# The state-space preparation on VectorE instead of GpSimd, a unit in three pieces

## The chip, the cores and the metric

The kernel runs on one core of a Trainium2 chip. The metric is the time of one execution on the device in microseconds (us), the median of three runs. The engines are named as in the profile: PE is TensorE (PEld its weight loads), DVE is VectorE, ACT is ScalarE, POOL is GpSimd, SP is SyncE, which here issues most DMAs.

## The reference, cut to what matters

The reference is a trunk of two layers over 512 latent and 256 context tokens of width 1024. Layer 0 mixes tokens by multi-head latent attention, layer 1 by a bidirectional S5 state-space layer; each is followed by a SwiGLU feed-forward network (FFN) of hidden width 2816:

```python
def swiglu(h, w_in, w_out):
    a, b = jnp.split(h @ w_in, 2, axis=-1)
    return (jax.nn.silu(a) * b) @ w_out

def s5_discretise(a_re, a_im, log_dt, b_re, b_im):
    dt = jnp.exp(log_dt.astype(f32))[:, None]
    mag = jnp.exp(dt * a_re)
    ab_re = mag * jnp.cos(dt * a_im)
    ab_im = mag * jnp.sin(dt * a_im)
    ...
    bb_re = f_re[..., None] * b_re - f_im[..., None] * b_im
    bb_im = f_re[..., None] * b_im + f_im[..., None] * b_re
    return ab_re, ab_im, bb_re, bb_im
```

The S5 layer of each direction is the scan h[t] = ab h[t-1] + bb u[t] (complex, 64 groups of 64 states and 16 channels), read out with the matrix c. The kernel doesn't scan token by token: it takes chunks of eight tokens, and needs for that, from the weights alone, matrices that hold the powers of ab times bb and c, and phases.

## The kernel before

**Order of the whole.** Attention of layer 0, its output product and norm, the first FFN (here FFN0, about 513 to 1166 us of the profile), the S5 mixer, a gated product (GLU), the second FFN.

**FFN0.** Function ffn works through the 22 tiles of the hidden width (ht) in five blocks of 5, 5, 4, 4 and 4 (BLOCKS). For each ht it makes two products (linear, tile f, each with a weight tile of 128x1024), then ACT takes the silu (tile sa), DVE multiplies (u), and ACT and DVE split u into a high and a low half (uh, ul). After a block come its eight output products (index m, tile fo), each added to x by DVE (residual, L801). Every product is made of three passes with high and low halves, so each weight is split first: ACT copies the high half (wh, L77), DVE subtracts for the low half (wl, L80). There are two buffers for the halves and two for the raw weights. The split of one weight is written two products ahead, so its buffer comes free when the product before the current one ends, and PE needs it when the current one ends.

**The preparation of the S5 matrices** rides along in FFN0. The generator hooks0 is advanced by next(hooks) once after each ht and after the output products m = 1, 4 and 6 (EXTRA): 37 times. Its first 28 steps (HOOKS) advance two generators: s5_prep (25 steps) and ada_rest (17 steps of modulation weights; a step is 32 small products on PE, tile ada). Then the pool pp of the preparation is closed, the S5 parameters of the first two k-tiles are loaded (s5_params, about 6 MB), ada_rows runs, and last the first GLU weights are loaded and split.

**s5_prep.** Four steps compute exponentials, sines and powers on DVE (tables apr, api, hr, hi, gr, gi with 64 columns per power). Then come 16 units, (kt, d) for eight k-tiles and two directions. A unit in elements:

- seven small DVE instructions on 128x64 (L1281 to L1289) make bb from the loaded tile bc (load, L1275, three buffers, one unit ahead);
- POOL copies bb into a block-diagonal tile bd (four copies, L1293);
- three complex outer products by outer (L1262 to L1267: four products, one difference, one sum each): w (128x512) on DVE, v (128x512) and en (128x384) on POOL.

All three use the same two intermediate tiles, ot0 and ot1, with one buffer each. One operand of each product is read from a power table with a step of 64 elements:

```python
ps = [qp(z[:, 0:8, cs] if d else z[:, 0:8, cs][:, ::-1, :]) for z in (apr, api)]
...
outer(nc.gpsimd, [bc[:, 2], bc[:, 3]], ps, (16, 8), v, True)
```

One unit later matrices transposes w on PE (tile wt) and multiplies v with bd (tile kps); w and v have two buffers each, so unit n+2 can't fill them before PE has done matrices of unit n. Further steps store en, v and the matrices to DRAM, read one back turned (toeplitz, eight DMAs on SP), turn it on ACT and store it.

**What sets the order.** A planner (schedule_with_timeline_sim) puts each engine's instructions into a fixed order when the program is built. It takes what is ready by its own estimate of times, and of what is ready the instruction that stands first in the program. The engines then run their queues in that order, each waiting for what its next instruction needs.

Of the kernel before, what the change touches and what calls it, by code (L numbers as in the profile page):

```python
# [10 lines left out]
F32 = mybir.dt.float32  # L11
F32R = mybir.dt.float32r
AF = mybir.ActivationFunctionType
# [4 lines left out]
P = 128  # L18
# [7 lines left out]
SKEW = 2  # L26
SHARE = (4, 4, 3)

EXTRA = (1, 4, 6)
QUADS = 10  # L30
LASTS = 2
HOOKS = 28
APART = (0, 1)
EARLY = (1, 2, 3, 4, 5, 6, 7, 8)

# [14 lines left out]
def trunk_kernel(ctx: ExitStack, tc: tile.TileContext, ins: dict, outs: dict):  # L50
    nc = tc.nc
# [194 lines left out]
    def ada_rows(pool_, f0, f1, n_):  # L246

        cb = pool_.tile([P, D], F32, tag="ada_c", name=f"ada_c{f0}")
        nc.sync.dma_start(cb, ins["cl"].broadcast_to([P, D]))
        nc.scalar.activation(cb, cb, AF.Silu)  # L250
        ws = {}

        def fetch(f):
            if f < f1:
                ws[f] = pool_.tile([P, D], F32, tag="ada_t", name=f"adat_{f}", bufs=n_)
                nc.sync.dma_start(ws[f], ins["ada_t"][f - 24])

        for f in range(f0, f0 + n_):
            fetch(f)
        yield  # L260
        for a in range(f0, f1, n_):
            for f in range(a, min(a + n_, f1)):
                w = ws.pop(f)
                tc.keep_in_program_order(nc.vector.scalar_tensor_tensor(
                    w, w, 1.0, cb, op0=ALU.mult, op1=ALU.mult, accum_out=mods[1][:, f, 0:1]))
                fetch(f + n_)
            if a + n_ < f1:
                yield
        m = mods[1][:, f0:f1, 0:1]
        nc.vector.tensor_add(m, m, ada_b[:, 1, f0:f1].unsqueeze(2))  # L270
        if f0 == 24:
            a = amods[3][:, :, 0:1]
            nc.vector.tensor_scalar_add(a, mods[1][:, 32:40, 0:1], 1.0)
            nc.vector.tensor_mul(a, a, gnorm[:, 3].unsqueeze(2))
        yield
# [109 lines left out]
    with pool("pa") as pa:  # L385
# [119 lines left out]
        for i in range(NT):  # L505
# [3 lines left out]
            z = zfirst[i] if i < FIRST else ps2(f"z{i}")  # L509
# [26 lines left out]
    with pool("pc") as pc:  # L536
# [193 lines left out]
        ada = ada_tasks(0, range(4, QUADS), lambda name: raw_tile("w_raw", name))  # L730
# [89 lines left out]
    def linear(accs, w, ops, n=KT):  # L820
        for k in range(n):
            passes(accs, w, ops, k, k, k == 0, k == n - 1)
# [29 lines left out]
    def ffn(layer, parts, pf, first, ops, hooks, norm=None, ahead=None):  # L852
        blocks = BLOCKS[layer]
        n = parts[-1][2]
        ub = max(b - a for a, b in blocks)
        gate = mod(layer, 5)
        for bi, (b0, b1) in enumerate(blocks):
            uh = pf.tile([P, ub, n], F32R, tag="uh", name=f"uh{layer}_{bi}")
            ul = pf.tile([P, ub, n], F32R, tag="ul", name=f"ul{layer}_{bi}")
            uops = [(part_of(uh, p_), part_of(ul, p_)) for p_ in parts]  # L860
            for ht in range(b0, b1):
                if ht == 0:
                    firsts = first()
                if ht < len(firsts):
                    ab = firsts[ht]
                else:
                    ab = accs_for(parts, f"f{layer}_{ht}", 2)
                    for acc in ab:
                        linear(acc, stream.take(), ops)
                sa = pf.tile([P, n], F32, tag="sa", name=f"sa{layer}_{ht}", bufs=1)  # L870
                u = pf.tile([P, n], F32, tag="u", name=f"u{layer}_{ht}", bufs=1 + layer)
                for acc, accb, (_, a, b) in zip(*ab, parts):
                    nc.scalar.activation(sa[:, a:b], acc, AF.Silu)
                    nc.vector.tensor_mul(u[:, a:b], accb, sa[:, a:b])
                split(uh[:, ht - b0, :], ul[:, ht - b0, :], u)
                next(hooks, None)
            for m in range(KT):
                w = stream.take()
                acc, = accs_for(parts, f"fo{layer}_{bi}_{m}")
                linear(acc, w, uops, b1 - b0)  # L880
                for z, p_ in zip(acc, parts):
                    residual(z, p_, m, gate)
                if m in EXTRA:
                    next(hooks, None)
                if norm is not None and b1 == HT:
                    norm.add(m, x[:, m, :])
                    if m == 3:
                        ahead()
                if layer and b1 == HT:
                    nc.sync.dma_start(outs["out"][:, m, :], x[:, m, :NL])  # L890
# [7 lines left out]
    with pool("pd") as pd:  # L898
# [18 lines left out]
        with pool("wx") as wx:  # L917
            tiles = [lambda nm, n, p_=p_: p_.tile([P, T], F32, tag="sq", name=nm, bufs=2)[:, :n] for p_ in (pd, wx)]
            more["pool"] = wx
            for p_, op in zip(PARTS, o_ops):  # L920
# [21 lines left out]
                bc = norm.bcast()  # L942
# [4 lines left out]
        with pool("pf0") as pf:  # L947
# [7 lines left out]
            pp = right.enter_context(pool("pp", side="right"))  # L955

            def hooks0():
                prep = s5_prep(nc, const, pp, ps1, ins, ident, views["s5_d"], views["i16"], sp)
                ada = ada_rest(pp)
                for j in range(HOOKS):  # L960
                    for _ in range(25 * (j + 1) // HOOKS - 25 * j // HOOKS):
                        next(prep, None)
                    next(ada, None)
                    yield
                assert next(prep, None) is None and next(ada, None) is None
                right.close()
                pq_ = right.enter_context(pool("ps5w", side="right"))
                mix["pool"] = pq_
                mix["params"] = s5_params(nc, pq_, sp)
                for kt in range(2):  # L970
                    mix["params"](kt)
                with pool("rows", side="right") as pv:
                    yield from ada_rows(pv, 24, 40, 3)
                pq_ = right.enter_context(pool("ps5v", side="right"))
                mix["w0"] = []
                for j in range(2):
                    raw = load(ins["s5_w_glu"][0, j], KT * P, f"wg0_0_{j}")[0]
                    w = [pq_.tile([P, KT * P], F32R, tag=f"w0{c}{j}", name=f"w0{c}{j}") for c in "hl"]
                    split_by(nc.gpsimd, *w, raw)
                    mix["w0"].append(w)  # L980
                    yield

            def ahead():

# [41 lines left out]
    with pool("pg") as pg:  # L1026
# [36 lines left out]
        with pool("ph", side="right") as ph, ExitStack() as wx:  # L1063
# [4 lines left out]
            for p_ in HALVES:  # L1068
                _, a, b = p_
# [30 lines left out]
def s5_prep(nc, const, pp, ps1, ins, ident, dsk, i16, sp):  # L1100
# [9 lines left out]
    V = nc.vector  # L1110
# [105 lines left out]
    hr, hi = new((P, 9, n), "hr"), new((P, 9, n), "hi")  # L1216
# [54 lines left out]

    def load(kt, d):

        bc = made["bc", kt, d] = pp.tile([P, 4, 4, 16], F32, tag="bc", name=f"bc{kt}_{d}", bufs=3)
        nc.sync.dma_start(bc, ins["s5_bc"][kt, d])  # L1275

    def elements(kt, d):

        cs = slice(32 * d + 4 * kt, 32 * d + 4 * kt + 4)
        bc = made["bc", kt, d]  # L1280
        ts(bc[:, 3], bc[:, 3], -1.0, None, op0=ALU.mult)  # L1281
        b3, t3 = ([new((P, 4, 16), f"{x}{c}") for c in range(2)] for x in ("bb", "bt"))
        f3 = [z[:, cs].unsqueeze(2).to_broadcast([P, 4, 16]) for z in (fr, fi)]
        tt(t3[0], bc[:, 0], f3[0], ALU.mult)
        tt(t3[1], bc[:, 1], f3[1], ALU.mult)
        tt(b3[0], t3[0], t3[1], ALU.subtract)
        tt(t3[0], bc[:, 1], f3[0], ALU.mult)
        tt(t3[1], bc[:, 0], f3[1], ALU.mult)
        tt(b3[1], t3[0], t3[1], ALU.add)  # L1289
        bd = bds[d]  # L1290
        for c in range(2):
            for g in range(2):
                nc.gpsimd.tensor_copy(bd[c][64 * g : 64 * g + 64, :, 16 * g : 16 * g + 16],  # L1293
                                      b3[c][64 * g : 64 * g + 64])

        ps = [qp(z[:, 0:8, cs] if d else z[:, 0:8, cs][:, ::-1, :]) for z in (apr, api)]
        w = made["w", kt, d] = [new((P, 4, 16, 8), f"w{c}", 2) for c in range(2)]
        outer(V, b3, ps, (16, 8), w)

        ps = [qp(z[:, 1:9, cs][:, ::-1, :] if d else z[:, 1:9, cs]) for z in (apr, api)]  # L1300
        v = made["v", kt, d] = [new((P, 4, 16, 8), f"v{c}", 2) for c in range(2)]
        outer(nc.gpsimd, [bc[:, 2], bc[:, 3]], ps, (16, 8), v, True)

        en = made["en", kt, d] = new((P, 2, 4, 12, 8), "en")
        outer(nc.gpsimd, [qp(z[:, :, cs]) for z in (gr, gi)], [qp(z[:, 0:8, cs]) for z in (hr, hi)], (12, 8),
              [en[:, 0], en[:, 1]])

    def store(kt, d):
# [66 lines left out]
            nc.sync.dma_start(sp["t"][kt], made.pop(("to", kt)).rearrange("p g c t -> p (g c t)"))  # L1375

    units = [(kt, d) for kt in range(KT) for d in range(2)]
    load(*units[0])
    yield

    line = [(5, store_turned), (4, turn), (3, toeplitz), (2, store_matrices), (1, store), (-1, load), (1, matrices), (0, elements)]
    for n_ in range(len(units) + 5):
        for lag, f in line:
            if 0 <= n_ - lag < len(units):
                f(*units[n_ - lag])
        yield


def s5_params(nc, pq, sp):
# [275 lines left out]
```

## Time and profile before

| what | value |
|---|---|
| median of 3 runs | 1765.08 us (1756.75 to 1771.79) |
| profiled execution | 1765.18 us, span from first to last instruction 1763.4 us |
| mean granted TensorE clock | 0.968 of full speed |
| busy in the span | PE 93%, PEld 80%, DVE 61%, ACT 39%, POOL 33% |

The profiled execution lies within 0.1 us of the median, so the sums below can be set against it directly. A busy share is a mean over stages; which engine holds up a stage is seen in the windows and in what PE waited for.

### The profile page before, as it was taken

Reading aid. Unit: us, or ns where it says so; the run is one execution under the profiler, and the core shown is the slowest. Engines: PE = TensorE matmul, PEld = TensorE weight load, DVE = VectorE, ACT = ScalarE, POOL = GpSimd, SP = SyncE. Lnnn points to the kernel's source line nnn. Section 1 sums busy time; section 2 is a strip of 40 time slices with the busy share of each in tenths; the row PEclk is TensorE's granted clock in tenths of the full one; section 3 lists DMA queues with packets and bytes.
Section 4 is the critical chain, followed back from the end, with each engine's and each line's share of the span. In section 5 each row is a group of like instructions: output and inputs, shape, how many; then the busy total and the mean of one; then the engine's idle time right before and its main releaser. Section 6 shows DMA issues by size and latency. Waiting matters only on the chain. (4 is left out here: it accounts for less than half of the span.)

```text
span 1763.4 us, 29083 instructions
## 1 busy us (share of the span) xinstructions
PE 1646.2 (93%) x11486; PEld 1406.3 (80%) x11486; DVE 1077.5 (61%) x1881; ACT 690.8 (39%) x1400; POOL 590.0 (33%) x626
## 2 busy tenths in 40 slices
PE   6979999999999999999989989976799999999999
PEld 5868878777888887877778878865579988888887
DVE  5787868787997356575566434547965654333332
ACT  3447757677453212222222312246525543232221
POOL 0156454510235247586667300046741100000000
PEclk9999989999999999999999999988879999999999
DMA  9130001124424355566435554353536452333231
GB/s 337 42 119 15 15 12 30 57 81 152 163 85 141 111 176 155 162 195 185 137 117 176 172 203 147 123 180 132 197 123 199 147 175 88 108 91 100 96 88 68
DMA packets 79832, 224.76 MB, mean 127 GB/s; under 512 B 8912, under 2 KB 24144, under 8 KB 77520
## 3 DMA queue, kind: packets, MB, share of 16 engines
q1 hardware_dynamic: 77472, 219.67, 38.4%
q10 hardware_dynamic: 2224, 3.24, 0.5%
q8 instruction: 90, 1.47, 0.3%
q14 instruction: 46, 0.38, 0.1%
HBM read 192.53 MB, written 30.34 MB: 126 GB/s over the span
## 5 line engine op out<-in xcount | busy, mean ns | idle before, releaser
L77 ACT ACTIVATE wh_wi<-wr_wi 128x1024 fp32r<-128x1024 f32 x88 | 93.2, 1061 | 321.6 <-PE f L818 259.5
L80 DVE TENSOR_TENSOR wl_wi<-wr_wi,wh_wi 128x1024 fp32r<-128x1024 f32 x88 | 116.3, 1323 | 130.4 <-ACT wh_wi L77 129.4
L818 PE MATMUL f<-hhh,wl_wi 128*128 128x512 f32 (+1 forms) x704 | 185.5, 341 | 5.0 <-DVE wl_wi L80 5.0
L818 PE MATMUL f<-hhl,wh_wi 128*128 128x512 f32 (+1 forms) x704 | 184.5, 340 | 0.0
L818 PE MATMUL f<-hhh,wh_wi 128*128 128x512 f32 (+1 forms) x704 | 183.7, 340 | 0.1
L818 PE MATMUL fo<-uh,wl_wo 128*128 128x512 f32 (+1 forms) x528 | 161.3, 361 | 9.0 <-DVE wl_wo L80 9.0
L818 PE MATMUL fo<-uh,wh_wo 128*128 128x512 f32 (+1 forms) x528 | 162.7, 364 | 4.3 <-ACT wh_wo L77 2.6
L818 PE MATMUL fo<-ul,wh_wo 128*128 128x512 f32 (+1 forms) x528 | 162.4, 361 | 3.4 <-DVE ul L80 3.4
L326 POOL TENSOR_TENSOR sqa<-sqa,sq 128x256 f32<-128x256 f32 (+2 forms) x25 | 37.9, 1515 | 323.3 <-ACT sq L324 321.5
L77 ACT ACTIVATE wh_wo<-wr_wo 128x512 fp32r<-128x512 f32 (+3 forms) x64 | 50.5, 793 | 239.9 <-PE fo L818 112.7
L818 PE MATMUL f<-hl_f,wh_wi 128*128 128x512 f32 (+1 forms) x384 | 142.8, 372 | 0.0
L818 PE MATMUL f<-hh_f,wl_wi 128*128 128x512 f32 (+1 forms) x384 | 142.6, 372 | 0.0
L818 PE MATMUL f<-hh_f,wh_wi 128*128 128x512 f32 (+1 forms) x384 | 142.1, 372 | 0.0
L801 DVE SCALAR_TENSOR_TENSOR x<-fo,mods,x 128x512 f32<-128x512 f32 x104 | 63.4, 644 | 120.4 <-PE fo L818 120.4
L818 PEld LDWEIGHTS f<-hhh,wl_wi 128*128 128x128 f32 x704 | 109.8, 190 | 21.0 <-DVE wl_wi L80 5.9
L818 PEld LDWEIGHTS f<-hhh,wh_wi 128*128 128x128 f32 x704 | 109.0, 189 | 17.1 <-issue 1.0
L818 PEld LDWEIGHTS f<-hhl,wh_wi 128*128 128x128 f32 x704 | 109.0, 189 | 15.7 <-issue 0.6
L818 PEld LDWEIGHTS fo<-uh,wl_wo 128*128 128x128 f32 x528 | 88.9, 192 | 24.0 <-DVE wl_wo L80 10.0
L818 PEld LDWEIGHTS fo<-uh,wh_wo 128*128 128x128 f32 x528 | 89.3, 193 | 19.7 <-ACT wh_wo L77 3.1
L818 PEld LDWEIGHTS fo<-ul,wh_wo 128*128 128x128 f32 x528 | 89.6, 193 | 18.6 <-DVE ul L80 4.3
L80 DVE TENSOR_TENSOR wl_wo<-wr_wo,wh_wo 128x512 fp32r<-128x512 f32 (+3 forms) x64 | 60.4, 947 | 55.1 <-ACT wh_wo L77 54.9
L709 ACT ACTIVATE pth<-pt 128x384 fp32r<-128x384 f32 (+1 forms) x160 | 71.8, 470 | 42.1 <-PE pt L705 40.7
(401 smaller groups left out, 4033.0 us busy)
## 6 DMA issues: line engine op xcount, KB each, us to landing
wr_wi<-ffn_w_in SPq DMA_DIRECT2D x88, 512.0 KB, 3.7
adaw<-ada_w SPq DMA_DIRECT2D x72, 512.0 KB, 4.5
wr_wg<-s_w_glu SPq DMA_DIRECT2D x30, 512.0 KB, 3.5
adat<-ada_t SPq DMA_DIRECT2D x24, 512.0 KB, 4.9
wr_wmo<-mla_w_o SPq DMA_DIRECT2D x16, 512.0 KB, 3.6
s_wout<-v SPq DMA_DIRECT2D x64, 128.0 KB, 2.6
s_win<-big SPq DMA_DIRECT2D x16, 512.0 KB, 4.8
s5win<-s_win SPq DMA_DIRECT2D x7, 1024.0 KB, 4.8
```

What stands on the lines that cost most here:

```text
L77: ins_ = nc.scalar.activation(hi, src, AF.Copy)
L80: eng.tensor_tensor(lo, src, hi.bitcast(F32), ALU.subtract)
L326: nc.gpsimd.tensor_tensor(self.acc, self.acc, sq, ALU.add)
L709: nc.scalar.activation(dh, pt3, AF.Copy)
L801: nc.vector.scalar_tensor_tensor(x[:, m, a:b], acc, gate[:, m, v : v + 1], x[:, m, a:b], op0=ALU.mult, op1=ALU.add)
L818: nc.tensor.matmul(acc, st, xs[lo][:, k, :], start=s, stop=e)
```

## The change

POOL leaves the units. The v and en outer products go to DVE, the four copies into bd to ACT. elements is cut into three functions, elements (small instructions, bd, w), readout (v) and phases (en), and each unit now takes three steps of the generator: s5_prep has 67 steps. FFN0 advances the hooks after each of the two products of an ht too, and after every m: 104 times, of which the first 73 advance the preparation. A step of ada_rest comes only with every fourth hook. bc gets a fourth buffer and is loaded two units ahead. After the preparation each step of ada_rows and of the first GLU weights takes three hooks.

```diff
-EXTRA = (1, 4, 6)
+EXTRA = ((0, 1, 2, 3, 4, 5, 6, 7), (1, 4, 6))
-HOOKS = 28
+HOOKS = 73
...
                     for acc in ab:
                         linear(acc, stream.take(), ops)
+                        if layer == 0:
+                            next(hooks, None)
...
-                if m in EXTRA:
+                if m in EXTRA[layer]:
                     next(hooks, None)
...
-                    for _ in range(25 * (j + 1) // HOOKS - 25 * j // HOOKS):
+                    for _ in range(67 * (j + 1) // HOOKS - 67 * j // HOOKS):
                         next(prep, None)
-                    next(ada, None)
+                    if j % 4 == 0:
+                        next(ada, None)
                     yield
...
-                    yield from ada_rows(pv, 24, 40, 3)
+                    for _ in ada_rows(pv, 24, 40, 3):
+                        for _ in range(3):
+                            yield
...
-                    yield
+                    for _ in range(3):
+                        yield
...
-        bc = made["bc", kt, d] = pp.tile([P, 4, 4, 16], F32, tag="bc", name=f"bc{kt}_{d}", bufs=3)
+        bc = made["bc", kt, d] = pp.tile([P, 4, 4, 16], F32, tag="bc", name=f"bc{kt}_{d}", bufs=4)
...
-                nc.gpsimd.tensor_copy(bd[c][64 * g : 64 * g + 64, :, 16 * g : 16 * g + 16],
-                                      b3[c][64 * g : 64 * g + 64])
+                nc.scalar.activation(bd[c][64 * g : 64 * g + 64, :, 16 * g : 16 * g + 16],
+                                     b3[c][64 * g : 64 * g + 64], AF.Copy)
...
+    def readout(kt, d):
+        cs, bc = slice(32 * d + 4 * kt, 32 * d + 4 * kt + 4), made["bc", kt, d]
...
-        outer(nc.gpsimd, [bc[:, 2], bc[:, 3]], ps, (16, 8), v, True)
+        outer(V, [bc[:, 2], bc[:, 3]], ps, (16, 8), v, True)
+
+    def phases(kt, d):
...
-        outer(nc.gpsimd, [qp(z[:, :, cs]) for z in (gr, gi)], [qp(z[:, 0:8, cs]) for z in (hr, hi)], (12, 8),
+        outer(V, [qp(z[:, :, cs]) for z in (gr, gi)], [qp(z[:, 0:8, cs]) for z in (hr, hi)], (12, 8),
...
-    load(*units[0])
+    for unit in units[:2]:
+        load(*unit)
     yield
-    line = [(5, store_turned), (4, turn), (3, toeplitz), (2, store_matrices), (1, store), (-1, load), (1, matrices), (0, elements)]
+    line = [[(5, store_turned), (4, turn), (3, toeplitz), (2, store_matrices), (1, store), (-2, load), (0, elements)],
+            [(1, matrices), (0, readout)], [(0, phases)]]
     for n_ in range(len(units) + 5):
-        for lag, f in line:
-            if 0 <= n_ - lag < len(units):
-                f(*units[n_ - lag])
-        yield
+        for part in line:
+            for lag, f in part:
+                if 0 <= n_ - lag < len(units):
+                    f(*units[n_ - lag])
+            yield
```

## Rows read from the trace of the kernel before

**Rows 1.** The page, part 1: busy time, share, instructions.

```profile
PE 1646.2 (93%) x11486; PEld 1406.3 (80%) x11486; DVE 1077.5 (61%) x1881; ACT 690.8 (39%) x1400; POOL 590.0 (33%) x626
```

**Rows 2.** Windows in FFN0: start:end, length, busy us, clock, DMA.

```profile
core 0: us, PE busy (x) PEld busy (x) DVE busy (x) ACT busy (x) POOL busy (x), PEclk, DMA share, GB/s
...
660.00:890.00 230.00, 217.40 (x1672) 185.67 (x1672) 145.71 (x209) 56.82 (x89) 161.33 (x142) 0.98 0.54 165
890.00:1000.00 110.00, 101.20 (x689) 85.40 (x688) 63.46 (x86) 28.07 (x43) 73.81 (x64) 0.97 0.50 150
1000.00:1040.00 40.00, 35.37 (x188) 30.02 (x188) 10.20 (x18) 10.32 (x15) 0.00 (x0) 0.91 0.70 272
1040.00:1140.00 100.00, 99.89 (x576) 87.91 (x575) 47.45 (x74) 20.27 (x29) 0.00 (x0) 1.00 0.40 129
545.00:1166.50 621.50, 594.72 (x4095) 510.61 (x4094) 334.22 (x486) 151.28 (x227) 300.69 (x259) 0.98 0.48 154
```

**Rows 3.** Waits between 545 and 1000: total us, times, longest.

```profile
DVE ot L1262 <- POOL en L1267: 62.8, 13, 9.5
DVE bc L1281 <- DMA bc<-s_bc: 26.9, 10, 7.0
```

**Rows 4.** Timeline around one stall, DVE's queue and PE.

```profile
790.37 1.08 DVE L1262 TENSOR_TENSOR ot<-bb,apr 128x512 f32<-128x512 f32 x1 [4.37 <-POOL en L1267]
...
795.21 0.20 DVE L1281 TENSOR_SCALAR bc<-bc 128x64 f32<-128x64 f32 x1 [2.04 <-DMA bc<-s_bc]
...
798.63 0.82 DVE L80 TENSOR_TENSOR wl_wo<-wr_wo,wh_wo 128x640 fp32r<-128x640 f32 x1
...
799.51 1.01 PE L818 MATMUL fo<-uh,wl_wo 128*128 128x512 f32 x2 [3.52 <-DVE wl_wo L80]
```

**Rows 5.** Groups by line and shape, 545 to 1000, DVE.

```profile
L80 DVE TENSOR_TENSOR wl_wi<-wr_wi,wh_wi 128x1024 fp32r<-128x1024 f32 x30 | 45.5, 1516 | 15.1 <-ACT wh_wi L77 15.1
L80 DVE TENSOR_TENSOR ul<-u,uh 128x768 fp32r<-128x768 f32 x15 | 22.5, 1500 | 0.2 <-ACT uh L77 0.2
L1289 DVE TENSOR_TENSOR bb<-bt,bt 128x64 f32<-128x64 f32 x15 | 15.0, 1003 | 0.7
```

**Rows 6.** Groups by line, 1040 to 1131, DVE; POOL idle throughout.

```profile
L80 DVE TENSOR_TENSOR wl_wi<-wr_wi,wh_wi 128x1024 fp32r<-128x1024 f32 x8 | 9.8, 1221 | 11.7 <-ACT wh_wi L77 11.7
L801 DVE SCALAR_TENSOR_TENSOR x<-fo,mods,x 128x512 f32<-128x512 f32 (+1 forms) x14 | 8.0, 613 | 17.0 <-PE fo L818 17.0
L80 DVE TENSOR_TENSOR wl_wo<-wr_wo,wh_wo 128x512 fp32r<-128x512 f32 x6 | 4.1, 684 | 2.2 <-ACT wh_wo L77 2.2
L874 DVE TENSOR_TENSOR u<-f,sa 128x512 f32<-128x512 f32 (+1 forms) x6 | 3.1, 554 | 18.4 <-PE f L818 18.4
L80 DVE TENSOR_TENSOR ul<-u,uh 128x768 fp32r<-128x768 f32 x3 | 2.9, 955 | 0.0
```

**Rows 7.** DVE's timeline while POOL stood idle: an outer product, small instructions.

```profile
872.26 1.08 DVE L1265 TENSOR_TENSOR ot<-bb,api 128x512 f32<-128x512 f32 x1
873.25 1.07 DVE L1266 TENSOR_TENSOR ot<-bb,apr 128x512 f32<-128x512 f32 x1
...
874.51 0.69 DVE L1267 TENSOR_TENSOR w<-ot,ot 128x512 f32<-128x512 f32 x1
875.11 0.26 DVE L1287 TENSOR_TENSOR bt<-bc,q 128x64 f32<-128x64 f32 x1
875.29 0.21 DVE L1288 TENSOR_TENSOR bt<-bc,q 128x64 f32<-128x64 f32 x1
```

**Rows 8.** The chain of waits, 1060 to 1135: start, us, what.

```profile
1065.29 66.29 PE f L818 x380
```

**Rows 9.** Groups by line and shape, 545 to 1000, PE: the preparation's products.

```profile
L1339 PE MATMUL kps<-v,bd 128*32 128x128 f32 x256 | 19.2, 405 | 1.0 <-POOL v L1267 0.9
L1330 PE MATMUL wt<-packed,w 128*128 128x128 f32 x128 | 17.3, 273 | 0.6 <-DVE w L1264 0.4 <-DVE w L1267 0.2
L171 PE MATMUL ada<-adaw,sc 128*32 128x128 f32 x400 | 14.0, 280 | 3.2 <-DVE mods L186 3.2
```

**Rows 10.** DVE's timeline, a GLU weight split ahead of FFN0's last residual.

```profile
1167.53 1.23 DVE L80 TENSOR_TENSOR wl_wg<-wr_wg,wh_wg 128x1024 fp32r<-128x1024 f32 x1 [3.87 <-ACT wh_wg L77]
1168.67 1.14 DVE L801 SCALAR_TENSOR_TENSOR x<-fo,mods,x 128x512 f32<-128x512 f32 x2
```

More of the change, by code (lines that the diff above doesn't have):

```diff
@@ L1298, in elements @@
         outer(V, b3, ps, (16, 8), w)
+    def readout(kt, d):
+        cs, bc = slice(32 * d + 4 * kt, 32 * d + 4 * kt + 4), made["bc", kt, d]
         ps = [qp(z[:, 1:9, cs][:, ::-1, :] if d else z[:, 1:9, cs]) for z in (apr, api)]
         v = made["v", kt, d] = [new((P, 4, 16, 8), f"v{c}", 2) for c in range(2)]
-        outer(nc.gpsimd, [bc[:, 2], bc[:, 3]], ps, (16, 8), v, True)
+        outer(V, [bc[:, 2], bc[:, 3]], ps, (16, 8), v, True)
+    def phases(kt, d):
+        cs = slice(32 * d + 4 * kt, 32 * d + 4 * kt + 4)
         en = made["en", kt, d] = new((P, 2, 4, 12, 8), "en")
-        outer(nc.gpsimd, [qp(z[:, :, cs]) for z in (gr, gi)], [qp(z[:, 0:8, cs]) for z in (hr, hi)], (12, 8),
+        outer(V, [qp(z[:, :, cs]) for z in (gr, gi)], [qp(z[:, 0:8, cs]) for z in (hr, hi)], (12, 8),
               [en[:, 0], en[:, 1]])
```

## The prediction, made before the change was run

> **What bounds the kernel now.** I read the busy shares first: PE is busy for 93% of the span [rows 1], so a change that leaves PE's products as they are can only win back PE's gaps, or add some. The windows then show where FFN0 has gaps. From 545 to 1166.5 us PE is busy for 594.72 of 621.5 us: 26.8 us of idle time, of which 12.6 lie between 660 and 890, 8.8 between 890 and 1000, 4.6 between 1000 and 1040, and nearly nothing after that [rows 2]. Those same stretches have a granted clock of 0.98, 0.97 and 0.91, so part of each ran at the lower of the two levels (1.2 instead of 2.4 GHz) after PE had stood still. Length times the missing share gives 4.6, 3.3 and 3.6 us, 11.5 us in all. FFN0's gaps therefore cost some 38 us. I take 38 as the most that this change can win there.
>
> What makes the gaps? In the waits between 545 and 1000, DVE stood 62.8 us at the first product of w until POOL had finished en of the unit before (they share ot0 and ot1), and 26.9 us for the DMA of bc [rows 3]. Neither wait is PE's, but DVE runs its queue in order, and weight splits stand behind them. One stall followed through: DVE waits 4.37 us for POOL at 790.37, then 2.04 us for bc at 795.21, reaches the split wl_wo at 798.63, and PE, 3.52 us idle, resumes at 799.51 [rows 4]. The second cost of POOL is contention. Small differences of 128x64 take 1003 ns on average where POOL works, against 0.2 us with POOL idle; the split wl_wi takes 1516 against 1221 ns, ul 1500 against 955 ns [rows 5 to 7]. So DVE is held up by POOL, PE by DVE.
>
> **What is removed.** Both waits go: v and en now follow w on the same engine, and bc is loaded a unit earlier with one more buffer. The contention goes: 30 x 0.295 = 8.9 us for wl_wi and 15 x 0.545 = 8.2 us for ul, and for the seven small instructions of a unit at least the 0.8 us of its last one, 12 us in 15 units. None of this is on the path by itself; it counts as room on DVE.
>
> **What is added to DVE.** With POOL idle, products of w start 0.99 us apart (872.26, 873.25), and the sum is followed by the next instruction after 0.60 us (874.51, 875.11) [rows 7]. An outer product of 128x512 is then 4 x 0.99 + 2 x 0.60 = 5.16 us. v has w's shape and reads the same tables, so 5.16. en isn't seen on DVE: it has 384 of 512 columns. By columns it is 3.87; if its strided operands are both slow it may be as dear as v, 5.16, and by columns without the slow reads 6 x 0.45 = 2.7. I take 3.87, because one operand of it is constant over the inner eight, as with w. Added per unit: 9.03 us (7.9 to 10.3), 144 us in 16 units.
>
> The slow products are where a page speaks against the row. A 512-column product of w takes 1.08 us, its sum with contiguous operands 0.69 [rows 7]. The Trainium skill, page "VectorE: DVE Perf Modes", section "Walkthrough: the 8-slice pipeline in each mode", says that in the plain mode any stride gives one result per cycle; by it all six instructions would cost like the sum. The trace contradicts it, and "SBUF — State Buffer", section "Door 1: The DMA port swizzle", fits it better: reads that leave a 16-byte line at each step pay a penalty. By the first page the added work would be 16 x (6 x 0.60 + 6 x 0.45) = 101 us, and the first rival below would be the forecast.
>
> **Does it fit?** A unit's whole DVE work is w, v, en and the small ones: 5.16 + 5.16 + 3.87 + seven small at 0.18 (875.11 to 875.29), 1.3, so 15.5 us. The first unit is written into hook 6, after the third ht, the last en into hook 57, the first m of block 3 (67 steps over 73 hooks). Between them lie 11 ht and 17 m.
>
> - PE: 11 ht at 66.29 / 4 = 16.6 us [rows 8] is 182. An m has 12 or 15 passes against 48 in an ht, so 4.1 or 5.2 us: 16 x 5.2 + 4.1 = 87. Transposes and kps of 16 units take 17.3 + 19.2 = 36, 13 ada steps at 14.0 / 12.5 = 1.1 us (400 products are 12.5 steps of 32) take 14 [rows 9]. Sum 319 us.
> - DVE: 16 x 15.5 = 248. Per ht two wl at 1.22, two u at 0.55 and ul at 0.96: 4.5; per m wl_wo and two x, 0.68 to 0.85 + 2 x 0.61: 2.0 [rows 6]. 11 x 4.5 + 17 x 2.0 = 84. Sum 332 us.
>
> So DVE would be about full for 320 us, 4% over. It starts ahead: from 545 us to hook 6 lie some 20 us with about 5 us of FFN work, so the planner can put about one unit there. Buffers limit the lead to two or three pieces. On average, then, it fits; but two engines that are both full can't wait for each other without loss. A split has about 6 us to spare within an ht (8.3 us of product less 1.06 + 1.2 us of ACT and DVE), one long piece. I take 10 us of idle PE for this stretch, and 4 us for the clock in the ratio of before (11.5 to 26.8): 14 instead of 12.6 + 4.6 = 17, a gain of 3.
>
> **The rest of FFN0.** After hook 57, about 890 us, DVE has no unit left, where the old kernel still had POOL's waits until 1000: the 8.8 + 3.3 us there go, 12. The stretch of 1000 to 1040 is the load of the S5 parameters, with DMA engines 70% busy [rows 2]. The pool pp now closes near the start of block 4, so that burst falls beside f products, whose weights have more time, instead of before fo. It may stall there too, so I count half of 4.6 + 3.6: 4. At FFN0's end the last x stood behind a GLU split until 1168.67 while PE was done at 1166.5 [rows 10]; with the first GLU weights five products earlier, 2 us go.
>
> **Edits with one answer.** ACT's copies into bd have no row of that shape; at no more than a 512-column instruction's 0.68 us [rows 6] they add 2.7 us a unit, and ACT has 173 of 230 us free [rows 2]. But each waits for bb, and weight splits stand behind it on ACT. bb is seven small instructions at the head of DVE's piece, so I count nothing; if DVE runs late, ACT's splits are late by the same time. SP has no more DMAs than before, in other places; ada's weights spread out, which relieves it. POOL's absence costs nothing. The S5 mixer, GLU and FFN1 stay as they are.
>
> **Forecast**: 3 + 12 + 4 + 2 = 21 us from 1765.2, 1744 us (1734 to 1756, if the first stretch loses 4 to 26 us instead of 14).
>
> **Rivals.**
>
> *DVE keeps up without loss.* All of FFN0's gaps go and nothing comes in: 38 + 2 us, 1725 us. For it: from 1040 to 1140, with DVE half busy, PE stood still for 0.1 us [rows 2]. Against: DVE isn't half busy but full. It needs a unit of some 11 us, as it would be without slow reads (12 x 0.60 + 6 x 0.45 + 1.3).
>
> *The gain is given back on the spot.* Pieces come bunched: a planner that thinks a product cheaper than 0.99 us packs more of them ahead of a split than PE's time covers. With DVE halfway to its upper bound (378, below), 355 us, PE waits 355 - 319 - 15 = 21 us, with clock 30, against 17 before: 13 lost, 18 won elsewhere, 1760 us. That the three pieces don't come where the hooks are, because the planner moves them, is the same case.
>
> *DVE becomes the bound: slower.* The place is the ht products of blocks 2 and 3: pieces of past hooks stand first in the program and go before the split. With en at 5.16 and every large instruction at its full duration instead of its spacing (18 x 0.09 = 1.6 us), a unit is 18.4 us and DVE needs 378: PE waits 378 - 319 - 15 = 44 us, with clock 63, against 17; less 18 elsewhere 1793 us. The point from which this turns slower than before is a loss of 35 us, idle 25, a unit of 17.2 us; by 1% from 17.9.
>
> **How the numbers follow.** Chances: forecast 0.42, no loss 0.18, given back 0.26, DVE bound 0.14. About 1% is what a measurement of this kernel tells from no change. Faster by over 1% (under 1747.4) takes the no-loss case and about two thirds of the forecast's own range: 0.46. Slower by over 1% (over 1782.7) is most of the last: 0.13. The remaining 0.41 is within 1%. The range runs from 1720, a little under the no-loss time, to 1783; beyond it are most of the last case and the outer ends of the sums.
>
> **What would show it.** Right: POOL nearly idle in 545 to 1000, no DVE waits for POOL or bc, small instructions at 0.2 us, DVE busy for over 85% of 570 to 880, products of v near 1.0 us; PE without a gap from 890 to 1000. Wrong: more than 25 us of idle PE before 890 with wl as its releaser (DVE full), ACT waiting for bb with wh splits behind it, en products over 1.1 us, or the parameter load stalling PE for longer than before.

## The result, and the profile after

The changed kernel takes 1740.7 us (median of 4 runs, 1739.4 to 1744.4) against 1763.4 us for the kernel before in the same comparison: a ratio of 0.987, 95% interval [0.984, 0.990], 1.3% faster. The profiled execution took 1739.5 us, 25.6 us less than that of before.

The page, part 1, of the changed kernel:

```profile
PE 1636.8 (94%) x11486; PEld 1398.1 (80%) x11486; DVE 1174.1 (68%) x2073; ACT 708.9 (41%) x1464; POOL 300.9 (17%) x370
```

DVE rises from 61% to 68%, POOL falls from 33% to 17% [rows 1]; PE has the same 11486 instructions. Windows of the changed kernel in FFN0 (start:end, length, busy us of each engine, clock, DMA):

```profile
core 0: us, PE busy (x) PEld busy (x) DVE busy (x) ACT busy (x) POOL busy (x), PEclk, DMA share, GB/s
660.00:890.00 230.00, 226.48 (x1816) 192.27 (x1815) 224.20 (x355) 73.98 (x141) 0.00 (x0) 1.00 0.63 194
890.00:1000.00 110.00, 107.96 (x727) 93.51 (x726) 36.62 (x60) 28.11 (x40) 0.00 (x0) 1.00 0.52 182
1000.00:1040.00 40.00, 37.15 (x214) 32.61 (x213) 24.04 (x41) 6.67 (x10) 0.00 (x0) 1.00 0.44 142
1040.00:1140.00 100.00, 99.57 (x575) 87.35 (x575) 44.24 (x67) 28.77 (x40) 14.62 (x11) 1.00 0.33 109
545.00:1142.10 597.10, 587.59 (x4159) 505.87 (x4160) 433.28 (x685) 169.23 (x289) 14.62 (x11) 1.00 0.51 162
```

From 660 to 890 DVE is busy for 97% of the time, and PE stands still for 3.5 us there, against 12.6 with DVE at 63% [rows 2]. The granted clock is 1.00 in all these stretches (down to 0.91 before). From the start of its first product (tile f) to the start of the last matmul of its output products, FFN0 runs from 512.9 to 1166.3 us before and from 514.9 to 1141.6 us now, 653.4 against 626.7 us. These 26.7 us are the whole gain of the profiled execution, which came to FFN0 2.0 us later.

DVE's groups by line and shape, 545 to 1000 (x count, busy us, mean ns, idle before):

```profile
L80 DVE TENSOR_TENSOR wl_wi<-wr_wi,wh_wi 128x1024 fp32r<-128x1024 f32 x33 | 40.2, 1219 | 18.9 <-ACT wh_wi L77 18.9
...
L1271 DVE TENSOR_TENSOR ot<-bc,api 128x512 f32<-128x512 f32 x16 | 17.3, 1080 | 0.0
...
L80 DVE TENSOR_TENSOR ul<-u,uh 128x768 fp32r<-128x768 f32 x17 | 16.2, 954 | 1.6 <-ACT uh L77 1.6
L1271 DVE TENSOR_TENSOR ot<-gr,hi 128x384 f32<-128x384 f32 x16 | 14.3, 891 | 0.4
...
L1273 DVE TENSOR_TENSOR v<-ot,ot 128x512 f32<-128x512 f32 x16 | 11.0, 686 | 0.1
...
L1295 DVE TENSOR_TENSOR bb<-bt,bt 128x64 f32<-128x64 f32 x15 | 3.3, 219 | 0.0
```

wl_wi, ul and bb are back at the times they had without POOL [rows 5 to 7]. The products of v take 1.08 us like those of w, those of en 0.89. No row of DVE waits for POOL any more, and the wait for bc has fallen from 26.9 to 2.2 us. DVE's timeline shows how splits come through in time:

```profile
806.24 1.14 DVE L801 SCALAR_TENSOR_TENSOR x<-fo,mods,x 128x512 f32<-128x512 f32 x2
807.29 0.88 DVE L1271 TENSOR_TENSOR ot<-gr,hi 128x384 f32<-128x384 f32 x1
808.10 0.89 DVE L1272 TENSOR_TENSOR ot<-gi,hr 128x384 f32<-128x384 f32 x1
808.90 0.82 DVE L80 TENSOR_TENSOR wl_wo<-wr_wo,wh_wo 128x640 fp32r<-128x640 f32 x1
809.64 0.56 DVE L1273 TENSOR_TENSOR en<-ot,ot 128x384 f32<-128x384 f32 x1
```

The split wl_wo stands inside en's outer product, ahead of its last sum. The queue is mixed by instructions, not by pieces or units, so a split has one product of about 1 us ahead of it. Two gaps of before's kind are left in 660 to 890 (PE's timeline):

```profile
752.92 1.08 PE L171 MATMUL ada<-adaw,sc 128*32 128x128 f32 x32 [1.92 <-DVE mods L186]
784.45 0.62 PE L818 MATMUL fo<-uh,wl_wo 128*128 128x512 f32 x2 [1.55 <-DVE wl_wo L80]
```

The largest gap of FFN0 now is a new one, 2.85 us at 1016. The chain of waits there (start, us, what):

```profile
1011.98 3.50 DVE adat L264 x6
1015.48 0.61 DVE wl_wo L80
1016.10 0.04 issue
1016.14 3.96 PE fo L818 x21
```

Three instructions of ada_rows (adat, each with a read of its accumulator) stand in front of a split.

### The profile page after: what moved, and what is told of

Read it like the earlier page. It is cut to its first block, busy times and chain, and to the rows that moved or that the text cites. A ratio compares the mean times of both kernels' runs of the same rounds, so it can differ in the third digit from the quotient of the medians.

```text
span 1737.8 us, 29048 instructions
## 1 busy us (share of the span) xinstructions
PE 1636.8 (94%) x11486; PEld 1398.1 (80%) x11486; DVE 1174.1 (68%) x2073; ACT 708.9 (41%) x1464; POOL 300.9 (17%) x370
## 4 chain that ended last, share of the span: by engine, by line
PE 70%; DVE 18%; issue 5%; ACT 3%; POOL 2%; DMA 2%; SPq 0%; DVEq 0%; POOLq 0%; ACTq 0%
PE f L818 33%; PE fo L818 13%; PE gl L818 5%; PE s L682 4%; PE pt L705 2%; PE kv L570 2%; DVE s5g L1510 2%; PE ada L171 1%; PE z L462 1%; PE oFalse L718 1%; PE oFalse L719 1%; PE q L597 1%; PE z L461 1%; DVE x L801 1%; DVE ot L1269 1%
## 5 line engine op out<-in xcount | busy, mean ns | idle before, releaser
L77 ACT ACTIVATE wh_wi<-wr_wi 128x1024 fp32r<-128x1024 f32 x88 | 93.1, 1060 | 317.9 <-PE f L818 236.9
L80 DVE TENSOR_TENSOR wl_wi<-wr_wi,wh_wi 128x1024 fp32r<-128x1024 f32 x88 | 107.4, 1222 | 130.6 <-ACT wh_wi L77 129.7
L818 PEld LDWEIGHTS f<-hhh,wh_wi 128*128 128x128 f32 x704 | 107.9, 188 | 18.1 <-ACT wh_wi L77 2.6
L80 POOL TENSOR_TENSOR w0l<-wr_wg,w0h 128x1024 fp32r<-128x1024 f32 x2 | 4.8, 2408 | 580.2 <-ACT w0h L77 580.2
```

The lines of the kernel that those rows point to most:

```text
L77: ins_ = nc.scalar.activation(hi, src, AF.Copy)
L80: eng.tensor_tensor(lo, src, hi.bitcast(F32), ALU.subtract)
L818: nc.tensor.matmul(acc, st, xs[lo][:, k, :], start=s, stop=e)
```

## The experiments

**Theory**: DVE's waits for POOL and the contention of the two engines held up the splits; with POOL out of the units both go, and DVE has just enough room. **Rivals**: that the cut into pieces and the denser hooks do it; that the waits alone, or the contention alone, were the cost; that a full DVE costs PE time; that another order would have given the same.

In the table, "FFN0" is the time in the profiled execution from the start of FFN0's first product to the start of the last matmul of its output products (both ends in brackets), and "idle" the time in which PE isn't busy from that first start to 0.5 us after the last. The length is compared and not the end alone, because the executions reach FFN0 at different times: e10 is there 6.0 us before the changed kernel, after the same instructions in the same order on every engine. So a few us between two profiles, outside the stretch looked at, say nothing of the edit.

| kernel | us (runs) | ratio to before [95%] | FFN0 | idle |
|---|---|---|---|---|
| before | 1763.4 | 1 | 653.4 (512.9 to 1166.3) | 27.9 |
| changed | 1740.7 (4) | 0.987 [0.984, 0.990] | 626.7 (514.9 to 1141.6) | 10.6 |
| e1 own tiles | 1779.9 (6) | 1.009 [1.006, 1.011] | 665.4 (516.9 to 1182.3) | 36.4 |
| e2 engines only | 1734.4 (4) | 0.983 [0.981, 0.985] | 625.6 (511.7 to 1137.3) | 8.4 |
| e3 pieces only | 1762.7 (11) | 0.999 [0.997, 1.001] | 653.6 (513.1 to 1166.7) | 30.2 |
| e4 changed, no step | 1743.3 (6) | 0.987 [0.984, 0.990] | 627.0 (513.6 to 1140.6) | 8.5 |
| e5 = e2, no step | 1726.5 (5) | 0.978 [0.976, 0.981] | 617.7 (513.4 to 1131.1) | 4.1 |
| e6 = e2, copies on POOL | 1737.3 (6) | 0.984 [0.981, 0.987] | 629.7 (511.7 to 1141.4) | 11.3 |
| e7 changed, en twice | 1778.5 (6) | 1.008 [1.005, 1.011] | 670.8 (509.6 to 1180.4) | 38.4 |
| e8 changed, old hooks | 1731.7 (6) | 0.982 [0.979, 0.984] | 622.5 (513.8 to 1136.3) | 6.2 |
| e9 = e2, POOL aside | 1853.2 (4) | 1.051 [1.049, 1.053] | 744.7 (512.7 to 1257.4) | 94.0 |
| e10 changed, old tail | 1732.0 (5) | 0.983 [0.981, 0.986] | 627.5 (508.9 to 1136.4) | 8.4 |
| e11 = e8, no step | 1734.7 (5) | 0.984 [0.981, 0.987] | 619.0 (512.6 to 1131.6) | 3.5 |
| e12 before, no step | 1736.2 (4) | 0.986 [0.984, 0.988] | 623.9 (512.4 to 1136.3) | 8.5 |

### Which part of the change: e2 and e3

e2 is the kernel before with v, en and the copies moved, and nothing else.

```diff
-                nc.gpsimd.tensor_copy(bd[c][...], b3[c][...])
+                nc.scalar.activation(bd[c][...], b3[c][...], AF.Copy)
...
-        outer(nc.gpsimd, [bc[:, 2], bc[:, 3]], ps, (16, 8), v, True)
+        outer(V, [bc[:, 2], bc[:, 3]], ps, (16, 8), v, True)
...
-        outer(nc.gpsimd, [qp(z[:, :, cs]) for z in (gr, gi)], ...
+        outer(V, [qp(z[:, :, cs]) for z in (gr, gi)], ...
```

> The kernel before with v and en on DVE and the bd copies on ACT, but still one piece a unit, 37 hooks, bc with three buffers. If leaving POOL is the whole of the gain, 1740 to 1745 us. If the three pieces and the denser hooks are needed, because 15 us of one unit stand ahead of a weight split that has 6 us to spare, PE waits 15 us or more for wl and wh and the time is 1750 to 1765.

e3 is its complement, the changed kernel with v, en and the copies back on POOL.

> The changed kernel with v, en and the bd copies back on POOL; 104 hooks, three pieces, four bc buffers stay. If POOL is the cause, DVE waits for en again (over 40 us) and the time is 1752 to 1768. If the order was the cause, 1740 to 1748.

e2 is 1.7% faster than before, below the range of either expectation, and e3 can't be told from before. So the move of the engines is the whole gain, and what comes with it adds nothing. Whether it costs something isn't settled: the changed kernel's median stands 6 us behind e2's, but the intervals touch, and FFN0 takes 626.7 and 625.6 us. In e3 DVE waits for POOL as before, and more:

```profile
DVE ot L1268 <- POOL en L1273: 82.8, 15, 8.0
```

### Waits or contention: e1 and e9

In the trace of before the path by way of the waits can be seen at more stalls than one. Three of PE's gaps, each with the wait of DVE ahead of it:

```profile
686.33 1.02 DVE L1262 TENSOR_TENSOR ot<-bb,apr 128x512 f32<-128x512 f32 x1 [6.66 <-POOL en L1267]
688.47 1.49 PE L171 MATMUL ada<-adaw,sc 128*32 128x128 f32 x32 [3.22 <-DVE mods L186]
...
878.78 0.20 DVE L1281 TENSOR_SCALAR bc<-bc 128x64 f32<-128x64 f32 x1 [3.01 <-DMA bc<-s_bc]
881.50 0.61 PE L818 MATMUL f<-hhh,wl_wi 128*128 128x512 f32 x2 [3.11 <-DVE wl_wi L80]
...
916.88 0.63 DVE L1281 TENSOR_SCALAR bc<-bc 128x64 f32<-128x64 f32 x1 [7.01 <-DMA bc<-s_bc]
922.00 1.01 PE L818 MATMUL fo<-uh,wl_wo 128*128 128x512 f32 x2 [3.58 <-DVE wl_wo L80]
```

Of PE's seven gaps of over 1 us between 545 and 1000, six end within 8 us behind such a wait of 2 us or more. They hold 18.1 of the 20.8 us of all gaps there. What follows asks whether it is enough to take the waits away.

e1 is the kernel before with one intermediate tile for each engine instead of two shared ones; the other product is formed in the output tile.

```diff
-        t1, t2 = (pp.tile(full, F32, tag=f"ot{j}", ...) for j in range(2))
+        own = "ot1" if eng is nc.gpsimd else "ot0"
+        t2 = pp.tile(full, F32, tag=own, ...)
         orr, oi = tiles
-        eng.tensor_tensor(t1, ar, br, ALU.mult)
+        eng.tensor_tensor(orr, ar, br, ALU.mult)
         ...
```

> The kernel before, but each outer product keeps one intermediate of its own engine (DVE ot0, POOL ot1) and forms the other product in the output tile, so w need not wait for POOL's en of the unit before. POOL keeps v, en and the copies, hooks and pieces are those of before. If the waits of DVE's queue for POOL are what cost (62.8 us in 13 waits), they go and PE's idle time from 660 to 1000 falls from 21 to about 10 us, 1750 to 1755 us. If it is the contention of the two engines, it stays or grows, since they now overlap more, and the time stays at 1760 to 1766.

It is slower than before, and beyond both ranges. DVE's wait for en is gone from its waits, and of PE's ten gaps of over 1 us only one still has a wait of DVE for bc within 8 us ahead of it; but the two engines now overlap more, and the gaps come to 34.7 us. e1's windows, and DVE's groups from 545 to 1000:

```profile
660.00:890.00 230.00, 213.30 (x1680) 180.82 (x1679) 201.28 (x208) 55.84 (x87) 200.49 (x150) 0.96 0.55 168
890.00:1000.00 110.00, 94.33 (x626) 80.12 (x629) 69.00 (x84) 26.69 (x40) 73.70 (x62) 0.92 0.44 135
```

```profile
L80 DVE TENSOR_TENSOR wl_wi<-wr_wi,wh_wi 128x1024 fp32r<-128x1024 f32 x30 | 52.4, 1746 | 18.0 <-ACT wh_wi L77 18.0
L1264 DVE TENSOR_TENSOR ot<-bb,api 128x512 f32<-128x512 f32 x16 | 32.4, 2024 | 0.4
```

DVE is busy for 201 us instead of 146 between 660 and 890 [rows 2]. The wait for en had kept w and POOL's products apart; without it a product of w takes up to 2.02 us on average instead of 1.08. The planner also orders the engines' queues otherwise from about 494 us on, so the time isn't that of the waits alone; the longer instructions are.

e9 is e2 with work on POOL that no engine waits for:

```diff
+        side = pp.tile([P, 4, 8, 8], F32, tag="side", ...)
+        a = qp(gr[:, 0:8, cs]).unsqueeze(3).to_broadcast([P, 4, 8, 8])
+        b = qp(hr[:, 0:8, cs]).unsqueeze(2).to_broadcast([P, 4, 8, 8])
+        for _ in range(18):
+            nc.gpsimd.tensor_tensor(side, a, b, ALU.mult)
```

> e2 (v, en and nothing else of the units left on POOL, old hooks) with work on POOL that nobody waits for: after each unit 18 products of 128x256 from the power tables into a tile of POOL's own, some 0.9 us each, 16 us a unit, about what v and en took there (12 instructions of 1.07 to 1.67 us, 16.4 us a unit). The values are not used. No engine waits for POOL, so this is contention alone. Theory (contention is the greater part of what POOL cost): DVE's small instructions go from 0.2 to about 1 us, products of w and v from 1.08 to 1.4 us or more; with v and en also on DVE the unit goes far beyond 17 us, and the gain of e2 over the kernel before (31 us) is lost: 1765 to 1800 us. Rival (the waits for POOL were the cost): DVE's instructions lengthen by some 10%, under 10 us of PE: 1734 to 1744 us.

It takes 119 us more than e2, beyond the theory's range. The planner's order differs from e2's from 527 us on, so this time too holds more than contention. But no engine waits for POOL's products for more than 0.2 us, and the same 752 instructions of DVE in FFN0 are busy for 585 us instead of 458. That makes contention enough to undo the change. The number is no price of what POOL did before: POOL works here nearly without a break from 533 to 901 us, and DVE is full of v and en as well. DVE's timeline while POOL's queue of products runs:

```profile
719.92 0.21 DVE L1288 TENSOR_TENSOR bt<-bc,q 128x64 f32<-128x64 f32 x1
720.06 1.67 DVE L1265 TENSOR_TENSOR ot<-bc,api 128x512 f32<-128x512 f32 x1
721.64 1.67 DVE L1266 TENSOR_TENSOR ot<-bc,apr 128x512 f32<-128x512 f32 x1
723.24 0.86 DVE L1289 TENSOR_TENSOR bb<-bt,bt 128x64 f32<-128x64 f32 x1
724.02 0.68 DVE L1267 TENSOR_TENSOR v<-ot,ot 128x512 f32<-128x512 f32 x1
```

What is added isn't in proportion to an instruction's length: of these five, one of 128x64 keeps its 0.21 us, the next takes 0.65 more, a product 0.59 more, the sum nothing. (Other sums do grow: on average from 545 to 1000 those of w take 1.02 us here and those of v 0.88, against 0.69.) The Trainium skill, page "SBUF — State Buffer", section "SBUF: two separate sides", describes this as a port pair of the two engines that one instruction holds as a whole while the other engine waits; additions of that kind agree with it, though POOL's times are too rough here to pair each one with a POOL instruction, and e6 below, where POOL alone becomes slower, agrees less.

### The copies: e6

e6 is e2 with the copies into bd left on POOL.

> e2 with the four copies into bd back on POOL, where they took 495 ns each in the kernel before, 30 us in all. Theory: a little work on POOL beside DVE costs what it overlaps, 4 x 0.5 us a unit, which slows a few of DVE's instructions by some 0.5 us: idle PE grows by under 2 us, 1734 to 1737 us. Rival 1: POOL's presence at all is what costs, and the gain over the kernel before shrinks by a third or more: 1745 us. Rival 2: the copies on ACT delay ACT's splits, and without them it is faster than e2: 1730 us.

1737.3 us; its ratio and that of e2 overlap, so the copies' place isn't told apart in the time. POOL's and DVE's groups in e6:

```profile
L1293 POOL COPY bd<-bb 64x64 f32<-64x64 f32 x60 | 51.5, 858 | 341.3 <-PE kps L1342 281.3 <-DVE u L874 20.5 <-DVE bb L1286 20.0
```

```profile
L80 DVE TENSOR_TENSOR wl_wi<-wr_wi,wh_wi 128x1024 fp32r<-128x1024 f32 x32 | 39.0, 1220 | 18.4 <-ACT wh_wi L77 18.4
...
L1289 DVE TENSOR_TENSOR bb<-bt,bt 128x64 f32<-128x64 f32 x15 | 3.3, 219 | 0.0
```

POOL's copies grow from 495 to 858 ns beside a busy DVE, while DVE's instructions stay at their undisturbed times (459 us of DVE in FFN0, 458 in e2). It is POOL's products, not every instruction of POOL, that slow DVE.

### The price of a full DVE: e4, e5, e7

In e4 the power tables lie the other way round, so that the products read them without a step. Its instructions stand in the same order on every engine as in the changed kernel; only their durations differ.

```diff
-    apr, api = new((P, 9, n), "apr"), new((P, 9, n), "api")
+    turned = lambda m, tag: new((P, n, m), tag).rearrange("p q x -> p x q")
+    apr, api = turned(9, "apr"), turned(9, "api")
...
-    hr, hi = new((P, 9, n), "hr"), new((P, 9, n), "hi")
-    gr, gi = new((P, 12, n), "gr"), new((P, 12, n), "gi")
+    hr, hi = turned(9, "hr"), turned(9, "hi")
+    gr, gi = turned(12, "gr"), turned(12, "gi")
```

> The changed kernel with the power tables stored so that the eight powers of a column lie side by side (views unchanged, so the inner step of the products is one element instead of 64). If the step is what makes products slow, they fall from 1.08 to 0.69 us (512) and 0.89 to 0.56 (384), 73 us of DVE work less. If the full DVE still costs PE time, idle PE from 545 to 1140 falls from 9.5 to 5 or less and the time to 1733 to 1737. If a full DVE does no harm, the time stays at 1738 to 1743.

A product and a sum of e4, and its windows:

```profile
L1274 DVE TENSOR_TENSOR w<-ot,ot 128x512 f32<-128x512 f32 x16 | 11.0, 687 | 0.5
L1269 DVE TENSOR_TENSOR ot<-bc,apr 128x512 f32<-128x512 f32 x16 | 11.0, 686 | 0.1
```

```profile
513.00:545.00 32.00, 28.86 (x226) 22.94 (x225) 31.69 (x73) 17.08 (x34) 5.66 (x5) 0.95 0.36 113
660.00:890.00 230.00, 230.00 (x1843) 196.18 (x1842) 176.99 (x353) 73.94 (x142) 0.00 (x0) 1.00 0.62 197
```

The step was the cause of the slow products. 47 us less DVE work close PE's 3.5 us in that stretch; making the tables costs more from 513 to 545, where PE has 28.86 instead of 30.88 us, and a gap of that kind stays at the split behind adat. The time is the same, and so is FFN0 (627.0 and 626.7 us).

e5 makes the same edit to e2, again with the order unchanged.

> The kernel before with v and en on DVE and the copies into bd on ACT (as in e2, whole units, old hooks), and with the power tables laid out so that the products of the outer products read them without a step, as in e4. Products should fall from 1.08 to 0.69 us (512 columns) and from 0.89 to 0.55 us (384). Theory: what e2 still loses (about 5.8 us of idle PE between 660 and 890, 0.8 ms further none) is splits behind a DVE that is 91% busy, so most of it goes: 1728 to 1731 us, ratio to e2 0.996 to 0.998. Rival: e2's remaining idle time is bound by transfers and by the order, not by DVE, as e4 gained nothing at the end over the changed kernel: 1734 us.

It is the fastest version, 1726.5 us, with PE busy without a gap from 545 to 1000. That is 2 us beyond the theory's range and rules out its rival. e11 (e8 with the same edit) has almost the same FFN0 in its profile, 619.0 against 617.7 us, but its times spread from 1726.9 to 1742.1 us, and the profiled execution is the fastest of them.

> e8 (units in three pieces, old hooks) with the power tables read without a step, as in e4 and e5. If pieces and whole units come to the same, it is as e5, 1726 us; if pieces let the planner place the shorter work better, 1722 to 1724 us; if e4's failure to gain was the pieces' and not the hooks', 1731 us.

So pieces add nothing to e5. Whether e4's failure to gain was theirs is open: FFN0 gains 3.5 us over e8, but the median, 1734.7 us, is no better than e8's.

e7 makes en twice in the changed kernel.

> The changed kernel with the outer product en made twice into the same tile, the second with the same values: 4 x 0.89 + 2 x 0.56 = 4.7 us more DVE work a unit, 75 us in 16 units, a unit of some 21 us, above the 17.2 us from which the prediction called DVE the bound. Theory by the prediction's own sum: DVE needs 407 us between hooks 6 and 57 against 334 us of PE, so PE waits some 70 us and the kernel comes to 1820 to 1840 us. Rival: the place of the hooks doesn't bind, and the planner lets the units run on into the stretch from 890 to 1000, where DVE is busy for 36.6 of 110 us; then only what doesn't fit there is paid, and the kernel comes to 1745 to 1765 us.

1778.5 us lies between the two. Windows of e7:

```profile
660.00:890.00 230.00, 207.91 (x1537) 175.53 (x1536) 226.98 (x361) 61.77 (x115) 0.00 (x0) 0.93 0.54 167
890.00:1000.00 110.00, 102.01 (x751) 87.17 (x751) 77.24 (x119) 30.78 (x51) 0.00 (x0) 0.95 0.63 214
```

The last en moves from 893 to 953 us. DVE has 68 us more to do in FFN0 (530.6 less 462.5), 41 us of it from 890 to 1000, and PE loses 28 us to idle time and 16 us in longer busy time, with a clock of 0.97 instead of 1.00. DVE goes from 97% to 99% busy between 660 and 890, and PE's idle time from 3.5 to 22.1 us: the limit is real and lies between the changed kernel's unit of about 16 us and e7's of about 20.

### What the layout costs: e8 and e10

e8 keeps the pieces and restores all hooks; e10 restores only those after the preparation.

```diff
-                    for _ in ada_rows(pv, 24, 40, 3):
-                        for _ in range(3):
-                            yield
+                    yield from ada_rows(pv, 24, 40, 3)
...
-                    for _ in range(3):
-                        yield
+                    yield
```

> The changed kernel with the old hooks: it is advanced 37 times as before, 28 of them for the preparation, which still comes in three pieces a unit (67 steps in 28 hooks); ada_rest at every hook and ada_rows and the first GLU weights one step a hook, as before. Theory: what the changed kernel loses against e2 comes from the late hooks, which put the parameter load, ada_rows and its adat copies beside other output products (its stalls at 961 and 1016), so it goes: 1733 to 1736 us. Rival: it comes from cutting the units into pieces or from bc two units ahead: 1740 us.

> The changed kernel with ada_rows and the first GLU weights one step a hook again instead of one in three; everything else as changed. e8, with all old hooks, was 9 us faster than the changed kernel. Theory: that loss is the tail's (stalls at 961 to 963 and 1016, and 3 us behind FFN0's end), so it is 1732 to 1736 us. Rival: it comes from the denser hooks or the rarer steps of ada_rest, and it stays at 1739 to 1742 us.

Both medians lie 9 us below the changed kernel's, with intervals that just overlap. What these loops cost isn't shown by the profiles. In e10 the gap of 2.85 us at 1016 is gone, but FFN0 takes 627.5 us against 626.7; its profile is ahead by the 6.0 us with which it came to FFN0, ahead of anything that the edit changed. In e8 FFN0 is 4.2 us shorter, but e8 restores the other hooks as well. Behind FFN0, from its end to the first GLU product, 126.3 us pass in the changed kernel and 123.6 in e10; in the other kernels it is 123.7 to 127.7, with the old loops or the new.

### Another way to the same gain: e12

e12 makes e4's edit to the kernel before. v and en stay on POOL.

> The kernel before, with the power tables read without a step and nothing else changed. w on DVE should cost 4 x 0.39 = 1.6 us less a unit where POOL stands still, 25 us of DVE in all; POOL's products may shorten too. Theory: with POOL's contention and waits left in place PE gains little: 1758 to 1765 us. Rival: the step also makes the two engines collide longer, and shorter products halve the contention: 1745 to 1752 us.

The theory is wrong, and the time lies below even the rival's range: 1736.2 us, near the changed kernel with the old hooks. Yet DVE's waits (total us, times, longest) are hardly shorter than in [rows 3], 81 against 90 us, and bb is still slow, so the contention isn't halved throughout:

```profile
DVE bc L1282 <- DMA bc<-s_bc: 40.6, 11, 9.6
DVE ot L1263 <- POOL en L1268: 40.4, 13, 8.2
```

```profile
L80 DVE TENSOR_TENSOR wl_wi<-wr_wi,wh_wi 128x1024 fp32r<-128x1024 f32 x33 | 44.9, 1359 | 22.8 <-ACT wh_wi L77 22.8
...
L1290 DVE TENSOR_TENSOR bb<-bt,bt 128x64 f32<-128x64 f32 x15 | 13.3, 885 | 1.0
```

Products fall from 1.08 to 0.69 us on DVE, and POOL's from 1.42 to 1.67 down to 1.17 to 1.37; wl_wi takes 1359 instead of 1516 ns. Here, unlike in e4 and e5, the planner also gave PE, DVE, ACT, POOL and SP another order. Of the waits, 81 us long, few reach PE: its gaps of over 0.25 us from 545 to 1000 come to 4.4 us, against 20.8 before. How much is the shorter products and how much the order is open.

## Why the prediction was right, point by point

The forecast was 1744 us; the time is 1740.7, and the case is the forecast's own. The sum of 21 us is 26.7 in FFN0: the first stretch gave far more than its 3 us, the other terms about what was counted or less. That the whole kernel, with 22.7 us, comes so near to 21 is in part luck. From FFN0's first product to its end PE's idle time fell from 27.9 to 10.6 us, and its busy time, for the same products, from 626.0 to 616.6.

- **What bounds the kernel**: right that PE's gaps in FFN0 are what can be won. The most, 38 us, was about right too: e5's FFN0 is 35.7 us shorter, with 4.1 us of idle time left, most of it before 545. Of the clock's 11.5 us the change got some 9.4, the fall of the busy time, with the clock at 1.00 throughout.
- **"DVE is held up by POOL, PE by DVE"**: right as a path. The stall that was followed [rows 4] stands for most of the sum: 18.1 of 20.8 us of gaps between 545 and 1000 come right behind a wait of DVE for POOL or bc. What the prediction left open, how much is the waits and how much the contention, stays open. e1 takes the largest wait away and the gaps grow, with longer instructions in place of waits; e9 shows contention enough to cost as much; e12 keeps waits of 81 us with hardly a gap. In the changed kernel both are gone at once.
- **Price of the added work**: v right (1.08 us a product, starts 0.99 apart). en's products start 0.80 us apart (807.29, 808.10), so with its sums, 0.56 long, an outer product is some 4.3 us where 3.87 was taken, inside the bounds. DVE is busy for 328 us from 545 to 890 (103.95 before 660, 224.20 after), against 332 forecast from hook 6 on, some 20 us later, and the last en ends at 893.
- **Loss of two full engines, 10 us of idle PE and 4 of clock**: the mis-sized term. From 545 to 890 PE stood still for 4.2 us and the clock was 1.00, so 8.4 us of idle time went where the prediction had 2.6 going. The step behind it, that a split waits behind "one long piece", was wrong: the queue is mixed by single instructions, so cutting the units did not matter either (e2, e8). Both sums of "Does it fit?" also left out a little, PE's the products kps<-bc,bd (8.2 us), DVE's adam, ed, e and mods (about 6 us), which leaves their balance as it was.
- **890 to 1000, gain 12**: the idle part was 6.8 (8.8 to 2.0) instead of 8.8. PE was not without a gap there: wh_wi came late once, for 1.75 us at 961.
- **Parameter load, gain 4**: idle 4.6 to 2.85, clock 0.91 to 1.00. The stall that is left isn't the load, as the prediction had it, but adat ahead of a split, and e10, whose order is the same until 990 us, doesn't have it: the tail's hooks put it there.
- **End of FFN0, gain 2**: not seen in the time. The last residual does come earlier, at 1141.89 us, 0.3 us behind the start of PE's last matmul instead of some 2. But from FFN0's end to the first GLU product (gl<-g,w0h) pass 125.4 us before and 126.3 after.
- **Edits with one answer**: the copies take 255 ns on ACT, not up to 680. ACT's wh_wo waited 5.6 us behind one for bb, without a gap of PE that names it. The rarer hooks of ada_rows and the GLU weights brought no gain that shows; without them the medians are 9 us lower (e8, e10), and where these 9 us lie isn't shown.
- **Rivals**: "no loss" (1725) was nearer in the first stretch than the forecast, for another reason than its condition: the unit isn't 11 us but about 16. e5, which meets the condition, gives 1726.5. "Given back on the spot" didn't come. "DVE bound" has the right mechanism and too high a price: e7's unit is above its turning point of 17.2 us, at about 20, and is slower than before by 0.8%, not by the 4% or so that the prediction's sum gives. That sum let the units end at hook 57; they ran on for 60 us into a stretch where DVE had room.

## What to carry to other kernels

An engine that is 97% busy off the critical path costs little if its queue is mixed by single instructions and its work may run on into a freer stretch; ask what has to be done by when before calling it the bound. Before moving work from one engine to another, look at how it reads memory: here a turned table alone, with the other order that the planner then chose, gave about as much as the move, and both together the most. A long wait in an engine's queue is a cause only if removing it helps; it can also be what keeps two engines out of each other's way.

## What the runs showed of the hardware

- A product of 128x512 takes 1.08 us on DVE when one operand is read with a step of 64 floats, and 0.69 us when the same values lie side by side; for 128x384 it is 0.89 and 0.55 (e4, e5). The Trainium skill's page "VectorE: DVE Perf Modes", section "Walkthrough: the 8-slice pipeline in each mode", by which the plain mode gives one result per cycle and takes any stride, does not hold here; e4 decides it by a change of layout alone.
- DVE and POOL, both at products of two operands, slow each other by up to twice: on DVE 2.02 us on average in e1 for a product of 1.08, on POOL up to 2.38 us before for one of 1.38 in the median. Copies of one operand on POOL leave DVE as it is and become slower themselves (858 against 495 ns, e6).
- DVE's instructions that read one operand from a product's tile (u from f, x from fo) aren't slowed by POOL in any of these runs: 687 and 747 ns for 128x512 before, 683 and 744 in e9, 686 and 748 in the changed kernel. Those that read two operands from tiles that PE doesn't write are, beside POOL's products: the split wl_wi takes 1516 ns before and 1553 in e9, and 1219 in the changed kernel.
